# Rounding v and scaling the probabilities on ScalarE in a two-layer hybrid decoder trunk

## Chip, core and metric

The kernel runs on one core of one Trainium2 chip. The metric is the device time of one execution in microseconds (us): 2591.58 us, the median of three runs (2588.98 to 2593.63).

The engines are named as in the profile: PE is TensorE (its weight loads are PEld), DVE is VectorE, ACT is ScalarE, POOL is GpSimd, SP is SyncE, which here issues nearly all DMAs. Each engine works through its own queue in order and waits on semaphores for the others.

## What is computed

Two decoder layers over 512 tokens of width 1024, all in float32. Each layer is a half-step feed-forward block, a token mixer and another half-step feed-forward block. The mixer has three branches, and the change lies in the first two:

```python
proj = h @ w_in                       # q, k, v for both kinds of heads, and u for the convolution
# A: 8 dilated heads of 64; q and k RMS-normed; one combined masked softmax
p = jnp.exp(logits - m)
o = jnp.einsum('...qk,...kc->...qc', p, v) / den
# B: 4 differential heads; two softmaxes for one v of 128
p = jax.nn.softmax(logits, axis=-1)
a = p[:, :, 0] - lam * p[:, :, 1]
out = jnp.einsum('bhqk,bhkd->bhqd', a, v)
# C: causal depthwise convolution with 31 taps over u, LayerNorm, swish
y = sum_i sigmoid(h @ w_gate_i + b_i) * (branch_i @ w_branch_i)
x = x + g2 * (y @ w_out)
```

## The kernel before

**Matmuls.** Every float32 product is made of three matmuls on rounded halves: each operand is split into a high part (rounded to fp32r) and a low part (operand minus high part), and high·high, low·high and high·low are added in PSUM. Weights come from HBM through SP into the buffers `wr`; ACT rounds them to `wh` (L226) and DVE subtracts to get `wl` (L230). Activations are split the same way (L268 on ACT, L269 on DVE).

**The mixer of a layer.** Eight groups `i` are worked one after the other: groups 0 to 3 hold two A heads each, groups 4 to 7 one B head each. They are called units here (unit 0 is group 0). `project` (L816) makes q, k and v of a unit: four PSUM banks `mm`, one per 128 tokens, with 96 matmuls each 384 wide. When a bank is complete, ACT copies its q and k to `qk` (L840), and v (128x128) is split into `v[:, 0]`, the rounded part (L841), and `v[:, 1]`, the rest (L842, on DVE). A bank can be reused by the next unit's projection only when L840, L841 and L842 have read it; there are four such banks. `qk_norm` then normalises q and k (DVE: L855 to L861).

**Attention** (`attention`, L908) handles a unit in four blocks of 128 queries, n = 0 to 3, each with w = 128 (n+1) keys. `scores` (L885) makes two score tiles, one per A head or one per softmax of a B head. DVE adds the bias and finds the maximum (L902), ACT takes the exponential in place and sums it into `den` (L904), and DVE takes the reciprocal `rd` (L920). In an A unit both tiles are multiplied by their reciprocals (L924). In a B unit the second reciprocal is first multiplied by minus lambda (L926), the second tile by that (L927), and the first tile is scaled and added (L928). After that PE transposes the tiles (L937), they are split into `pT` (L268, L269), and `pv` (L964) or `sc` (L979, L982) multiplies them with both parts of v.

**What runs beside it.** PE fills its time with the next unit's projection, `pull(n)` taking n matmuls of it at a time. Each pull also advances the convolution: 4 x 31 taps, each one DVE instruction on 128x512 (L770). For the first three of four channel groups one tap is issued every 4 pulls, for the last one every 14. All of it is written in program order and then put into a fixed order per engine when the program is built; on the chip each engine's queue is in that order.

Of the kernel before, what the change touches and what calls it, by code (L numbers as in the profile page):

```python
# [16 lines left out]
AF = mybir.ActivationFunctionType  # L17
ALU = mybir.AluOpType
# [55 lines left out]
class Trunk:  # L74
# [741 lines left out]
    def project(self, l, i, st):  # L816

        nc, io = self.nc, self.io
        ps = [self.bank("mm") for _ in range(4)]
        for sub in range(4):  # L820
            if sub == 3:
                st["qk"] = qk = self.t4k([P, 4, 256], F32, "qk")
                st["v"] = v = self.t4k([P, 2, 4, P], F32R, "v")
            w = self.weight("qkv", l, i, sub)
            for t in range(4):
                for kk in range(2):
                    k = sub * 2 + kk
                    hs = slice(t * P, (t + 1) * P)
                    ws = slice(kk * 384, (kk + 1) * 384)
                    hi, lo = self.h[k]  # L830
                    o = ps[t][:, 0:384]
                    nc.tensor.matmul(o, hi[:, hs], w[0][:, ws], start=k == 0, stop=False)  # L832
                    yield
                    nc.tensor.matmul(o, hi[:, hs], w[1][:, ws], start=False, stop=False)  # L834
                    yield
                    nc.tensor.matmul(o, lo[:, hs], w[0][:, ws], start=False, stop=k == KD - 1)  # L836
                    if k < KD - 1:
                        yield
                if sub == 3:
                    nc.scalar.activation(qk[:, t, :], ps[t][:, 0:256], AF.Copy)  # L840
                    nc.vector.tensor_copy(v[:, 0, t, :], ps[t][:, 256:384])  # L841
                    nc.vector.tensor_tensor(v[:, 1, t, :], ps[t][:, 256:384],  # L842
                                            v[:, 0, t, :].bitcast(F32), op=ALU.subtract)
                    if t == 3:
                        self.qk_norm(l, i, st)
                    yield
# [61 lines left out]
    def attention(self, l, i, st, ys, pull, before):  # L908
        nc = self.nc
# [5 lines left out]
        def sa(n):  # L915
            w = (n + 1) * P
            e0, e1 = self.scores(st, (0, 1), (0, 1) if A else (0, 0), n,
                                 (den[:, 2 * n:2 * n + 1], den[:, 2 * n + 1:2 * n + 2]), pull)
            rd = self.small(2, "rd")
            nc.vector.reciprocal(rd, den[:, 2 * n:2 * n + 2])  # L920
            if A:
                dat[n] = [e0, e1]
                for j, e in enumerate(dat[n]):
                    nc.vector.tensor_scalar(e[:, 0:w], e[:, 0:w], rd[:, j:j + 1], None, op0=ALU.mult)  # L924
                return
            nc.vector.tensor_tensor(rd[:, 1:2], rd[:, 1:2], self.neglam[:, l:l + 1], op=ALU.mult)  # L926
            nc.vector.tensor_scalar(e1[:, 0:w], e1[:, 0:w], rd[:, 1:2], None, op0=ALU.mult)  # L927
            nc.vector.scalar_tensor_tensor(e0[:, 0:w], e0[:, 0:w], rd[:, 0:1], e1[:, 0:w],  # L928
                                           op0=ALU.mult, op1=ALU.add)
            dat[n] = [e0]  # L930
# [96 lines left out]
        for n, upto in enumerate((24, 29, 48, 65, 77, 96) if A else (22, 40, 53, 63, 86, 108)):  # L1027
            if n < 4:
                sa(n)
            if n == 0 and before:  # L1030
                pull(13)
                before()
            if not A:
                pull(12)
            for j in range(2 if A else 1):
                if A and n in (3, 5) and j == 0:
                    pv(n // 2 - 1)
                if not A and 0 <= n - 2 < 4:
                    sc(n - 2)
                if 0 <= n - 1 < 4:  # L1040
                    left = base + upto - pull.count
                    pull(max(0, left // (4 - j) if A else left - 2))
                    sb(n - 1, j)
            pull_to(upto)
# [200 lines left out]
```

## Time and profile before

| | us |
|---|---|
| median of three runs | 2591.58 |
| the profiled execution | 2593.34 |
| its span, first to last instruction | 2591.2 |
| layer 0: units 0 to 3 (the A heads) | 478.3 to 618.6 |
| layer 1: units 0 to 3 | 1758.1 to 1900.1 |
| TensorE's mean granted clock, share of 2.4 GHz | 0.987 |

A unit is taken here from the start of its first L902 on 128x128 to that of the next unit's. The span holds two mixers of some 400 us each and four feed-forward blocks around them. A busy time is the time in which at least one instruction of the engine ran. Instructions of DVE and ACT overlap their successors a little, so the distance from one start to the next is somewhat shorter than a duration. The clock column of a stretch is a mean of two levels, 1.2 and 2.4 GHz.

### The profile page before, as it was taken

The page shows a single profiled execution, that of the slowest core. Times are in us where ns is not written, and L with a number is a line of the kernel's source. Part 1 is how long each engine was busy: PE and PEld are TensorE (multiplying, and loading weights), DVE is VectorE, ACT ScalarE, POOL GpSimd, SP SyncE. Part 2 cuts the span into 40 slices and gives each one's busy share as a digit, 9 for nine tenths or more (in the row PEclk, how much of TensorE's full clock was granted, in tenths as well). Part 3 has the DMA queues.
Part 4 walks back from the last instruction along what each step waited for, and adds up shares of the span by engine and source line. Part 5 has one row for each costly group of instructions (what it writes and reads, how often), then busy time and mean ns, then how long its engine had stood idle before and what let it go on. Part 6 is the DMA issues. An engine that isn't in the chain of part 4 may idle for free.

```text
span 2591.2 us, 37974 instructions
## 1 busy us (share of the span) xinstructions
PE 2505.5 (97%) x15072; PEld 2201.5 (85%) x15072; DVE 1968.4 (76%) x3519; ACT 1124.6 (43%) x1765; POOL 30.5 (1%) x33
## 2 busy tenths in 40 slices
PE   6899999989999999999989999999899999999999
PEld 4889898877778889898989898898787778898988
DVE  8988876989873468979678796679898744785855
ACT  4435343545562345343455353435455523552533
POOL 2000000000000000000000000000000000000000
PEclk9999999989999999999999999999899999999999
DMA  7474644212223323737324553331122232233332
GB/s 264 163 244 158 236 149 127 80 46 76 78 90 98 90 74 98 260 107 260 107 65 157 209 183 123 96 88 54 50 81 78 90 94 93 66 106 98 101 97 89
DMA packets 97747, 312.20 MB, mean 120 GB/s; under 512 B 10345, under 2 KB 17257, under 8 KB 97570
## 3 DMA queue, kind: packets, MB, share of 16 engines
q1 hardware_dynamic: 97424, 309.65, 37.1%
q8 instruction: 118, 1.93, 0.3%
q14 instruction: 59, 0.48, 0.1%
q10 hardware_dynamic: 146, 0.14, 0.0%
HBM read 307.62 MB, written 6.06 MB: 121 GB/s over the span
## 4 chain that ended last, share of the span: by engine, by line
PE 82%; DVE 12%; ACT 3%; issue 2%; DMA 1%; SPq 0%; DVEq 0%; ACTq 0%
PE mm L583 16%; PE mm L274 13%; PE mm L276 13%; PE mm L278 13%; PE s L583 12%; PE mm L834 3%; PE mm L832 3%; PE mm L836 3%; DVE wr L770 2%; PE s L895 2%; DVE wl L230 2%; DVE ada L431 1%; DMA ada<-in_w_ada 1%; PE o L964 1%; DVE hx L491 1%
## 5 line engine op out<-in xcount | busy, mean ns | idle before, releaser
L226 ACT ACTIVATE wh<-wr 128x1024 fp32r<-128x1024 f32 (+1 forms) x481 | 485.2, 1010 | 641.6 <-PE mm L278 303.0
L230 DVE TENSOR_TENSOR wl<-wr,wh 128x1024 fp32r<-128x1024 f32 (+1 forms) x468 | 544.7, 1166 | 238.3 <-ACT wh L226 237.1
L274 PE MATMUL mm<-ah,wh 128*128 128x512 f32 (+1 forms) x752 | 287.1, 383 | 0.0
L274 PE MATMUL mm<-hh,wh 128*128 128x512 f32 (+1 forms) x776 | 281.6, 366 | 5.7 <-ACT wh L226 2.9
L278 PE MATMUL mm<-al,wh 128*128 128x512 f32 (+1 forms) x752 | 286.7, 382 | 0.0
L276 PE MATMUL mm<-hh,wl 128*128 128x512 f32 (+1 forms) x776 | 281.5, 366 | 5.2 <-DVE wl L230 5.2
L276 PE MATMUL mm<-ah,wl 128*128 128x512 f32 (+1 forms) x752 | 286.4, 382 | 0.0
L583 PE MATMUL mm<-sh,wh 128*128 128x256 f32 x936 | 268.4, 287 | 16.6 <-ACT wh L226 13.9
L278 PE MATMUL mm<-hl,wh 128*128 128x512 f32 (+1 forms) x776 | 276.5, 367 | 7.2 <-DVE hl L500 7.1
L583 PE MATMUL mm<-sh,wl 128*128 128x256 f32 x936 | 268.0, 286 | 0.5 <-DVE wl L230 0.5
L583 PE MATMUL mm<-sl,wh 128*128 128x256 f32 x936 | 267.7, 286 | 0.0
L509 DVE SCALAR_TENSOR_TENSOR x<-mm,res,x 128x512 f32<-128x512 f32 (+1 forms) x124 | 86.2, 697 | 156.2 <-PE mm L278 156.0
L583 PEld LDWEIGHTS mm<-sh,wh 128*128 128x128 f32 x936 | 182.1, 195 | 18.6 <-ACT wh L226 14.7
L834 PE MATMUL mm<-wl,hh 128*128 128x384 f32 x512 | 183.8, 359 | 8.5 <-DVE wl L230 8.5
L832 PE MATMUL mm<-wh,hh 128*128 128x384 f32 x512 | 177.3, 360 | 8.7 <-DVE v L842 8.7
L583 PEld LDWEIGHTS mm<-sh,wl 128*128 128x128 f32 x936 | 182.5, 195 | 1.2 <-DVE wl L230 0.8
L836 PE MATMUL mm<-wh,hl 128*128 128x384 f32 x512 | 183.5, 358 | 0.0
L583 PEld LDWEIGHTS mm<-sl,wh 128*128 128x128 f32 x936 | 182.6, 195 | 0.0
L770 DVE SCALAR_TENSOR_TENSOR wr<-u,par,wr 128x512 f32<-128x512 f32 x240 | 176.1, 744 | 0.2
L431 DVE SCALAR_TENSOR_TENSOR ada<-ada,cb 128x1024 f32<-128x1024 f32 x144 | 173.1, 1219 | 3.1 <-DMA ada<-in_w_ada 2.9
L274 PEld LDWEIGHTS mm<-hh,wh 128*128 128x128 f32 x776 | 147.6, 191 | 32.5 <-ACT hh L493 4.1
L583 PE MATMUL s<-hl,wh 128*128 128x256 f32 x624 | 175.1, 281 | 0.0
(218 smaller groups left out, 5603.8 us busy)
## 6 DMA issues: line engine op xcount, KB each, us to landing
wr<-in_w_up SPq DMA_DIRECT2D x156, 512.0 KB, 3.7
ada<-in_w_ada SPq DMA_DIRECT2D x144, 512.0 KB, 5.7
wr<-in_w_down SPq DMA_DIRECT2D x64, 512.0 KB, 5.4
wr<-in_w_qkv SPq DMA_DIRECT2D x64, 384.0 KB, 3.2
wr<-in_w_gate SPq DMA_DIRECT2D x48, 512.0 KB, 3.7
wr<-in_w_down SPq DMA_DIRECT2D x32, 384.0 KB, 3.1
wr<-in_w_branch SPq DMA_DIRECT2D x24, 512.0 KB, 3.6
wr<-in_w_u SPq DMA_DIRECT2D x16, 512.0 KB, 3.6
```

The costliest lines, as they stand in the source:

```text
L226: nc.scalar.activation(hi[:, :n], raw[:, :n], AF.Copy)
L230: eng.tensor_tensor(lo[:, :n], raw[:, :n], hi[:, :n].bitcast(F32), op=ALU.subtract)
L274: nc.tensor.matmul(ps[:, rng], w[0][:, wcol], ah[:, rng], start=start, stop=False)
L276: nc.tensor.matmul(ps[:, rng], w[1][:, wcol], ah[:, rng], start=False, stop=False)
L278: nc.tensor.matmul(ps[:, rng], w[0][:, wcol], al[:, rng], start=False, stop=stop)
L431: nc.vector.scalar_tensor_tensor(w, w, 1.0, cb, op0=ALU.mult, op1=ALU.mult, accum_out=self.mod[l][:, e:e + 1])
L509: self.nc.vector.scalar_tensor_tensor(self.x[d][:, rng], ps[:, rng], self.res[l][:, 8 * s + d:8 * s + d + 1], self.x[d][:, rng], op0=ALU.m ...
L583: nc.tensor.matmul(o, w[a][:, c], acts[k][b], start=first and (mi, k, x) == (0, 0, 0), stop=(k, x) == (3, 2), skip_group_check=True)
L770: nc.vector.scalar_tensor_tensor(ca[j], u, w, ca[j], op0=ALU.mult, op1=ALU.add)
L832: nc.tensor.matmul(o, hi[:, hs], w[0][:, ws], start=k == 0, stop=False)
L834: nc.tensor.matmul(o, hi[:, hs], w[1][:, ws], start=False, stop=False)
L836: nc.tensor.matmul(o, lo[:, hs], w[0][:, ws], start=False, stop=k == KD - 1)
```

## The change

Three lines of code move from VectorE to ScalarE: the rounding of v to its high part (64 instructions of 128x128), the scaling of both A tiles by their reciprocals (64 instructions, 16 each of 128, 256, 384 and 512 columns), and the scaling of the second B tile (32 instructions, 8 of each width). The values computed are the same products and roundings.

```diff
                 if sub == 3:
                     nc.scalar.activation(qk[:, t, :], ps[t][:, 0:256], AF.Copy)
-                    nc.vector.tensor_copy(v[:, 0, t, :], ps[t][:, 256:384])
+                    nc.scalar.activation(v[:, 0, t, :], ps[t][:, 256:384], AF.Copy)
...
                 for j, e in enumerate(dat[n]):
-                    nc.vector.tensor_scalar(e[:, 0:w], e[:, 0:w], rd[:, j:j + 1], None, op0=ALU.mult)
+                    nc.scalar.activation(e[:, 0:w], e[:, 0:w], AF.Copy, scale=rd[:, j:j + 1])
                 return
             nc.vector.tensor_tensor(rd[:, 1:2], rd[:, 1:2], self.neglam[:, l:l + 1], op=ALU.mult)
-            nc.vector.tensor_scalar(e1[:, 0:w], e1[:, 0:w], rd[:, 1:2], None, op0=ALU.mult)
+            nc.scalar.activation(e1[:, 0:w], e1[:, 0:w], AF.Copy, scale=rd[:, 1:2])
```

Since the order per engine is made anew when the program is built, it moves in other places of the mixers too, on PE, DVE, ACT and (the bias loads `G`) SP. The number of table loads on ACT is 32 in both programs.

First, DVE in layer 0 at the end of unit 1, where the banks of unit 3's projection are emptied. `mm_4985` and `mm_4986` are the first two of its four banks, `v_5235` its v, `qT` the split q and k of unit 2, `wl` a weight's low part and the `wr` rows are taps of the convolution:

```order
 L881 SCALAR_TENSOR_TENSOR qT_5231<-s_5226,par,qT_5231 128x512
 L230 TENSOR_TENSOR wl_5239<-wr_5236,wh_5238 128x768
 L770 SCALAR_TENSOR_TENSOR wr_4357<-u_4103,par,wr_4357 128x512
-L841 CAST v_5235<-mm_4985 128x128
-L770 SCALAR_TENSOR_TENSOR wr_4357<-u_4103,par,wr_4357 128x512
 L842 TENSOR_TENSOR v_5235<-mm_4985,v_5235 128x128
 L770 SCALAR_TENSOR_TENSOR wr_4357<-u_4103,par,wr_4357 128x512
-L841 CAST v_5235<-mm_4986 128x128
-L770 SCALAR_TENSOR_TENSOR wr_4357<-u_4103,par,wr_4357 128x512
 L842 TENSOR_TENSOR v_5235<-mm_4986,v_5235 128x128
+L770 SCALAR_TENSOR_TENSOR wr_4357<-u_4103,par,wr_4357 128x512
```

The subtraction that frees the first bank stands behind one tap in place of a tap, the rounding and a second tap.

Second, ACT in unit 2 of layer 0, query blocks n = 1 (`p_5345`, `p_5349`) and n = 2 (`p_5392`, `p_5396`):

```order
 L904 ACTIVATE p_5349,den_5215<-p_5349,m_5350 128x256
 L268 ACTIVATE pT_5359<-s_5375 128x128
+L924 ACTIVATE p_5345<-p_5345,rd_5353 128x256
+L924 ACTIVATE p_5349<-p_5349,rd_5353 128x256
 L268 ACTIVATE pT_5359<-s_5409 128x2x128
 L904 ACTIVATE p_5392,den_5215<-p_5392,m_5393 128x384
 L268 ACTIVATE pT_5359<-s_5419 128x2x128
 L904 ACTIVATE p_5396,den_5215<-p_5396,m_5397 128x384
+L924 ACTIVATE p_5392<-p_5392,rd_5400 128x384
+L924 ACTIVATE p_5396<-p_5396,rd_5400 128x384
```

Two scalings now stand between a pair of exponentials and the next work of ACT; each waits for a reciprocal of DVE.

Third, DVE in the first B unit of layer 0 (unit 4, n = 0; `p_6016` and `p_6020` are the two softmaxes, `v_5977` is the v of the next unit):

```order
 L855 TENSOR_REDUCE ss_6043<-sq_6044 128x4
-L842 TENSOR_TENSOR v_5977<-mm_5742,v_5977 128x128
-L230 TENSOR_TENSOR wl_6082<-wr_6079,wh_6081 128x768
-L920 RECIPROCAL rd_6024<-den_5957 128x2
-L841 CAST v_5977<-mm_5743 128x128
-L926 TENSOR_TENSOR rd_6024<-rd_6024,neglam 128x1
 L855 TENSOR_REDUCE ss_6043<-sq_6047 128x4
-L927 TENSOR_SCALAR p_6020<-p_6020,rd_6024 128x128
-L842 TENSOR_TENSOR v_5977<-mm_5743,v_5977 128x128
 L928 SCALAR_TENSOR_TENSOR p_6016<-p_6016,rd_6024,p_6020 128x128
```

L928 now waits for ACT where it followed L927 on its own engine; the reciprocal and L926 have moved further ahead of it.

## Rows read from the trace of the kernel before

**Rows 1.** The page, busy time, share of the span and instructions of each engine:

```profile
PE 2505.5 (97%) x15072; PEld 2201.5 (85%) x15072; DVE 1968.4 (76%) x3519; ACT 1124.6 (43%) x1765; POOL 30.5 (1%) x33
```

**Rows 2.** Busy time by stretch, units 0 to 3 of layer 0:

```profile
core 0: us, PE busy (x) PEld busy (x) DVE busy (x) ACT busy (x) POOL busy (x), PEclk, DMA share, GB/s
478.30:509.00 30.70, 29.38 (x165) 24.31 (x164) 28.48 (x89) 18.46 (x48) 0.00 (x0) 1.00 0.17 51
509.00:547.30 38.30, 33.90 (x182) 27.80 (x183) 36.59 (x101) 18.24 (x49) 0.00 (x0) 0.96 0.18 50
547.30:589.60 42.30, 36.04 (x171) 29.61 (x170) 37.19 (x101) 16.67 (x46) 0.00 (x0) 0.86 0.17 50
589.60:618.60 29.00, 27.74 (x152) 23.09 (x153) 26.25 (x84) 15.17 (x43) 0.00 (x0) 0.96 0.22 63
```

**Rows 3.** The same columns, units 0 to 3 of layer 1:

```profile
1758.10:1788.80 30.70, 29.37 (x165) 24.33 (x164) 28.49 (x89) 18.49 (x48) 0.00 (x0) 1.00 0.18 51
1788.80:1827.10 38.30, 33.91 (x182) 27.83 (x183) 36.59 (x101) 18.12 (x49) 0.00 (x0) 0.96 0.17 50
1827.10:1869.60 42.50, 36.22 (x171) 29.76 (x170) 37.25 (x102) 16.68 (x46) 0.00 (x0) 0.86 0.17 49
1869.60:1900.10 30.50, 29.25 (x153) 24.52 (x154) 26.23 (x85) 15.20 (x43) 0.00 (x0) 0.90 0.21 61
```

**Rows 4.** Chain that ended last, 528 to 546 us: start, us, what:

```profile
528.54 0.79 DVE p L924 x2
...
543.06 0.87 DVE wl L230
543.92 0.66 DVE wr L770
544.59 0.20 DVE v L841
544.79 0.66 DVE wr L770
545.45 0.21 DVE v L842
```

**Rows 5.** PE in order of time: start, us, instruction, idle time before it and releaser:

```profile
545.80 0.66 PE L832 MATMUL mm<-wh,hh 128*128 128x384 f32 x1 [1.84 <-DVE v L842]
...
546.57 0.52 PE L836 MATMUL mm<-wh,hl 128*128 128x384 f32 x1
546.89 0.52 PE L832 MATMUL mm<-wh,hh 128*128 128x384 f32 x1
...
557.42 0.34 PE L834 MATMUL mm<-wl,hh 128*128 128x384 f32 x1
557.59 0.34 PE L836 MATMUL mm<-wh,hl 128*128 128x384 f32 x1
```

**Rows 6.** Busy time by stretch of L841 (first) and L924 (second) alone, unit 1:

```profile
509.00:547.30 38.30, 1.14 (x4) 0.96 0.18 50
...
509.00:547.30 38.30, 2.78 (x8) 0.96 0.18 50
```

**Rows 7.** Groups by line and shape: count, busy us, mean ns of one, idle before; last, line L924:

```profile
L841 DVE CAST v<-mm 128x128 fp32r<-128x128 f32 x64 | 17.5, 282 | 0.0
L904 ACT ACTIVATE p<-p,m 128x512 f32<-128x512 f32 x32 | 22.9, 716 | 3.2 <-DVE m L902 3.2
L904 ACT ACTIVATE p<-p,m 128x128 f32<-128x128 f32 x32 | 12.6, 395 | 22.6 <-DVE m L902 18.5 <-DVE rs L313 4.0
L268 ACT ACTIVATE pT<-s 128x128 fp32r<-128x128 f32 x40 | 10.9, 272 | 19.4 <-PE s L937 15.4 <-DVE pT L269 3.7
L226 ACT ACTIVATE wh<-wr 128x768 fp32r<-128x768 f32 x104 | 87.1, 843 | 155.7 <-PE mm L836 66.4 <-PE mm L278 38.3 <-issue 32.4
L924 DVE TENSOR_SCALAR p<-p,rd x64: 274/380/481, 481.7 to 1888.2; 128x128 f32<-128x128 f32 x16, 128x256 f32<-128x256 f32 x16, 128x384 f32<-128x384 f32 x16, 128x512 f32<-128x512 f32 x16
```

**Rows 8.** Busy time by stretch, units 4 and 5 of layer 0, and 690 to 700 us:

```profile
618.60:649.60 31.00, 31.00 (x181) 26.86 (x181) 29.50 (x98) 16.39 (x42) 0.00 (x0) 1.00 0.26 78
649.60:687.80 38.20, 38.19 (x202) 30.81 (x201) 36.08 (x113) 18.18 (x39) 0.00 (x0) 1.00 0.26 77
690.00:700.00 10.00, 8.55 (x42) 5.70 (x41) 8.25 (x22) 7.52 (x13) 0.00 (x0) 1.00 0.39 120
```

## Prediction

> **What bounds the kernel now.** I read the page's busy shares first: PE is busy 97% of the span and ACT 43% [rows 1]. Taken alone that says that a change on DVE and ACT is worth nothing. The share is an average, though, so the second view is the busy time of each unit of the mixer. In units 0 to 3 of layer 0 PE stands idle for 30.70-29.38 = 1.3, 38.30-33.90 = 4.4, 42.30-36.04 = 6.3 and 29.00-27.74 = 1.3 us, 13.2 us in all [rows 2]. In the same stretches the granted clock is 0.96 to 0.86 of 2.4 GHz in three of the four. A stretch of 38.3 us at a mean of 0.96 has lost 1.5 us of full-speed time, the others 5.9 and 1.2, together 8.6. Layer 1 repeats it: 13.2 us idle, and 1.5 + 6.0 + 3.1 = 10.6 us of clock [rows 3]. So these eight units lose 45.6 us of PE's time, and that is all that the change can win there; in units 4 and 5 PE has no gap at all [rows 8].
>
> Who holds PE up is read from DVE's column and from the chain. In units 1 and 2 DVE is busy 36.59 of 38.30 and 37.19 of 42.30 us, ACT less than half [rows 2]. The chain that ended last runs through DVE at the end of unit 1: two scalings, later a weight's low part, a tap, the rounding of v, another tap, the subtraction [rows 4]. Behind that PE has waited 1.84 us for L842, the last reader of a bank that the next projection needs. The wide matmuls after it start 0.32 us apart, where later ones start 0.17 apart [rows 5]: the wait costs a second time, as a stretch at 1.2 GHz. So DVE, with the taps on top of the attention, is the limit in units 1 and 2. In unit 3 the taps come at the slower rate, and DVE is busy 26.25 of 29.00 us.
>
> **What the change takes from DVE.** Per A unit four roundings and eight scalings go: 1.14 + 2.78 = 3.92 us of DVE busy time in unit 1 [rows 6]; the other units are within 0.2. That is the upper bound, since neighbours overlap. In the chain two scalings of 512 columns take 0.79 and a rounding 0.20 [rows 4], against 0.28 for the rounding's duration [rows 7], so about 0.08 of each of the 12 is overlap: the lower bound is 3.9-1.0 = 2.9. I take the middle, 3.4 us.
>
> **What ACT gets.** The trace has no multiplication by a column on ACT from SBUF to SBUF. The nearest row is the exponential in place with a column as its bias: 0.395 us at 128 columns, 0.716 at 512 [rows 7], the upper bound for this operation; a rounding of 128x128 from PSUM takes 0.272 there, and v's is the same. Eight scalings of 0.56 on average (half-way between the two) and four roundings are 4.4 + 1.1 = 5.5 us per A unit. ACT is busy 18.2 of 38.3 us in unit 1, so it would go to 23.7 us: it has the room. As engine time alone it costs nothing, covered by ACT's idle time, and where that cover is gone it is 5.5 us a unit.
>
> Here a rule speaks against the change. On DVE a scaling takes 0.27 to 0.48 us, and the row of an exponential in the same shape says 0.4 to 0.7 on ACT [rows 7]. The Trainium skill, "ScalarE: Activation LUTs", section "Rules for kernel authors", wants multiplications on VectorE, not ScalarE; the trace agrees that each one gets dearer. By that rule, ACT being the bound, each unit would lose some 5.5 us; by the row that DVE is the full engine it gains.
>
> **The sum.** The work that PE has in unit 1 is 38.3-4.4-1.5 = 32.4 us, in unit 2 42.3-6.3-5.9 = 30.1. DVE's work after the change is 36.6-3.4 = 33.2 and 37.2-3.4 = 33.8: still a little more than PE's, so DVE stays the limit of these two units, with less over. I leave it the 1.7 us of idle time it has in unit 1 now, waits for other engines, in both. The unit then takes 34.9 and 35.5 us: gains of 3.4 and 6.8 us. The second is larger because the slow clock, which makes DVE wait for PE now, goes with the long waits. Units 0 and 3 are bound by PE; of their 1.3 us of gaps each I take half, and unit 3's 1.2 us of slow clock in part: 0.7 and 0.8. Layer 0 gains 11.7 us. Layer 1 has the same units with 42.5 us in unit 2 (gain 7.0) and more slow clock in unit 3, which follows unit 2's waits (2.1): 0.7 + 3.4 + 7.0 + 2.1 = 13.2. Together 24.9.
>
> **What it adds.** In the A units the scaling waits on ACT for a reciprocal of DVE. Queued behind it on ACT are the copies of the transposed tiles, the next exponentials and, in places, `wh` and the copies of q, k and v; PE waits for all of them. In the new order the reciprocal stands right behind the exponentials, with a tap or less between, so I take this as covered by DVE's smaller backlog. The roundings go behind L840 in ACT's queue, and L842 waits for them in place of its neighbour; with 0.27 us each and two taps fewer in front of the first subtraction, nothing is added.
>
> In the B units, one scaling per block leaves DVE, and L928 waits for it there. DVE loses about 2 us of work per unit (four scalings and four roundings, half to two thirds of an A unit's), which is worth nothing where PE has no gap [rows 8]. Below, then, zero. Above, each of the 32 waits lasts a whole `wh` of 0.84 us and a scaling of 0.72 [rows 7], 6.2 us per unit; DVE's free time is 1.5 and 2.1 us in units 4 and 5 plus those 2 us, so some 2.5 us per unit would come through, 20 us over eight units. The new order puts other DVE work between L926 and L928, so I take the row near the bottom: 1 us per layer, at the place where PE already waits in this stretch (8.55 of 10 us, ACT 7.52 busy) [rows 8]. Table loads stay 32 and cost nothing new. The bias loads that SP issues in another order move by one weight load and are wanted a unit later: nothing.
>
> 24.9-2.0 = 22.9 us. Against the profiled execution's own 2593.3 us that is 2570.4; that execution stands 1.8 us above the median of the runs, so 2568.7, rounded **2569 us**.
>
> **The rivals.** First, **ACT's queue becomes the slow link** (slower). The place is the pair of scalings in each of the 32 blocks of A units, 16 per layer. If the reciprocal sits behind taps in DVE's backlog, ACT stands still at the scaling, and the copies that PE needs stand behind it. One tap is 0.66 us [rows 4]: at one per block 21 us, about the whole gain; at two 42 us, which gives 2570 + 42 = 2612, or 2611 in the median. It decides from 22.9/32 = 0.7 us per block. For it: the exponentials already wait mostly for DVE's maximum (18.5 of the 22.6 us before the 128-wide ones) [rows 7]. Against it: the reciprocal's place in the new order, and that the backlog is what shrinks. Chance 0.11. The Trainium skill's rule above is this case; the trace bears out its price per instruction, not that ACT is the bound.
>
> Second, **DVE's time is given back as waits**. L842 and L920 now wait for ACT more often; if DVE's idle time per unit grows by the 3.4 us that it was relieved of, units 1 and 2 stay at 38.3 and 42.3; units 0 and 3 still give 1.5 us a layer, the B units take 1: 2591, within 0.2%. For it: in unit 2 DVE is idle for 5.1 us now. Against: those lie in the slow-clock stretch. Chance 0.12.
>
> Third, **half of it**: unit 1 gains, but one wait of PE's in unit 2 stays long enough for the clock to fall as it does now, 5.9 us. Then a layer gains 3.4 + 0.9 + 1.5 = 5.8 us, less 1: 9.6 us in all, 2582. Chance 0.17.
>
> Fourth, **the whole loss goes**: the relief brings DVE's work under PE's everywhere, since over the four units it falls to 128.5-13.6 = 114.9 us against PE's 140.3-13.2-8.6 = 118.5. All 45.6 us: 2546; nine tenths of it, 2551. Chance 0.10. That the change doesn't do what it says can be left out: the three lines stand on ACT in the new order.
>
> **How the numbers follow.** The forecast, a gain of 13 to 33 us, has 0.50. A measurement of this kernel tells about 0.2%, 5.2 us, from no change. Faster: 0.50 + 0.17 + 0.10 = 0.77; within: 0.12; slower: 0.11. The range runs from 2552, leaving out some 0.07 below, to 2591, leaving out the slower case and a little of the second rival above.
>
> **What would show it.** In the changed profile DVE's busy time in units 1 and 2 of both layers should be near 33 to 34 us, PE's wait for L842 at the start of unit 2 gone, the granted clock at 0.98 or above there, and units 1 and 2 near 35 us. ACT should be near 24 us busy in them. A wait of ACT's for L920 of over 0.7 us per block would show the first rival; DVE waiting for L841 or L927 the second; a stretch with matmuls 0.32 us apart the third. PE below full in units 4 and 5 would show the B units' cost. The prediction is wrong if units 1 and 2 keep their lengths although DVE's work fell, or if the time goes in a place outside the A units.

## The result, and the profile after

The change takes 2561.02 us, the median of four runs (2559.45 to 2561.60), against 2592.28 us before (four runs, 2588.98 to 2593.63): a ratio of 0.988, 95% interval 0.9863 to 0.9897, or 31.3 us faster. The prediction was 2569 us in 2552 to 2591: right in its sign and its place, and too small by 8 us. The profiled execution of the changed kernel took 2559.45 us, with a span of 2557.4 and a mean granted clock of 0.995 of 2.4 GHz (before: 0.987).

The page's busy shares, to be read beside [rows 1]:

```profile
PE 2492.0 (97%) x15072; PEld 2188.8 (86%) x15072; DVE 1929.6 (75%) x3359; ACT 1177.0 (46%) x1925; POOL 30.5 (1%) x33
```

160 instructions have gone from DVE to ACT, 39 us of DVE's busy time has gone and 52 us of ACT's has come, and PE's share has not moved. The page alone still hides the change; the stretches show it. These are units 0 to 5 of layer 0 in the changed kernel, to be read beside [rows 2] and [rows 8]:

```profile
core 0: us, PE busy (x) PEld busy (x) DVE busy (x) ACT busy (x) POOL busy (x), PEclk, DMA share, GB/s
477.70:508.20 30.50, 30.33 (x170) 25.33 (x171) 27.35 (x79) 20.94 (x58) 0.00 (x0) 1.00 0.18 55
508.20:540.70 32.50, 32.50 (x178) 26.41 (x177) 30.23 (x84) 22.10 (x63) 0.00 (x0) 1.00 0.22 61
540.70:576.20 35.50, 32.03 (x179) 26.66 (x177) 34.47 (x90) 22.02 (x60) 0.00 (x0) 1.00 0.20 57
576.20:603.10 26.90, 26.82 (x146) 21.71 (x145) 23.95 (x73) 18.70 (x52) 0.00 (x0) 1.00 0.25 69
603.10:634.20 31.10, 31.10 (x180) 26.66 (x179) 29.28 (x89) 19.62 (x52) 0.00 (x0) 1.00 0.25 77
634.20:672.00 37.80, 37.24 (x198) 30.03 (x197) 35.80 (x110) 20.65 (x47) 0.00 (x0) 1.00 0.27 78
```

And units 1 to 3 of layer 1, beside [rows 3]:

```profile
1769.60:1802.10 32.50, 32.50 (x178) 26.42 (x177) 30.23 (x84) 22.12 (x63) 0.00 (x0) 1.00 0.23 61
1802.10:1837.60 35.50, 32.01 (x173) 26.68 (x172) 34.46 (x90) 22.00 (x60) 0.00 (x0) 0.96 0.19 56
1837.60:1865.90 28.30, 28.29 (x152) 23.21 (x152) 24.02 (x74) 18.72 (x52) 0.00 (x0) 0.98 0.25 67
```

Against before, units 0 to 3 of layer 0 are 0.2, 5.8, 6.8 and 2.1 us shorter, 14.9 together, and those of layer 1 0.2, 5.8, 7.0 and 2.2, 15.2 together: 30.1 of the 31.3 us lie in the A units. (The two profiled spans differ by 33.8; the executions profiled lie 2.5 us further apart than the medians.) In unit 1 PE has no gap left, in unit 2 still 3.5 us in each layer. Units 4 and 5 are as they were, to 0.4 us. A unit's start is a mark on DVE, and PE's order around it has changed too, so a tenth of a microsecond in such a difference means nothing.

At the start of unit 2, where PE waited 1.84 us for L842 [rows 5], nothing waits now. PE there, in order of time:

```profile
540.17 0.44 PE L832 MATMUL mm<-wh,hh 128*128 128x384 f32 x1
540.45 0.34 PE L834 MATMUL mm<-wl,hh 128*128 128x384 f32 x1
540.62 0.34 PE L836 MATMUL mm<-wh,hl 128*128 128x384 f32 x1
```

The matmuls start 0.17 us apart, the pace of 2.4 GHz, where [rows 5] had 0.32. DVE's queue just before, beside [rows 4]:

```profile
537.43 0.95 DVE L230 TENSOR_TENSOR wl<-wr,wh 128x768 fp32r<-128x768 f32 x1
538.30 0.74 DVE L770 SCALAR_TENSOR_TENSOR wr<-u,par,wr 128x512 f32<-128x512 f32 x1
538.96 0.28 DVE L842 TENSOR_TENSOR v<-mm,v 128x128 fp32r<-128x128 f32 x1
```

The first subtraction starts 1.53 us after the weight's low part; before it was 545.45 - 543.06 = 2.39 [rows 4]. The 0.86 us between them is the rounding (0.20) and the tap behind it (0.66). That turned out to be a large part of the story.

### The profile page after: what moved, and what is told of

Same layout as the page of the kernel before. It is cut to its first block, busy times and chain, and to the rows that moved or that the text cites. A ratio compares the mean times of both kernels' runs of the same rounds, so it can differ in the third digit from the quotient of the medians.

```text
span 2557.4 us, 37996 instructions
## 1 busy us (share of the span) xinstructions
PE 2492.0 (97%) x15072; PEld 2188.8 (86%) x15072; DVE 1929.6 (75%) x3359; ACT 1177.0 (46%) x1925; POOL 30.5 (1%) x33
## 4 chain that ended last, share of the span: by engine, by line
PE 86%; DVE 9%; ACT 2%; issue 1%; DMA 1%; DVEq 0%; ACTq 0%
PE mm L583 17%; PE mm L274 14%; PE mm L278 14%; PE mm L276 14%; PE s L583 13%; PE mm L836 3%; PE mm L834 3%; PE mm L832 3%; PE s L895 2%; DVE wl L230 1%; DVE wr L770 1%; PE o L964 1%; PE s L937 1%; DVE ada L431 1%; DVE hx L491 1%
## 5 line engine op out<-in xcount | busy, mean ns | idle before, releaser
L226 ACT ACTIVATE wh<-wr 128x1024 fp32r<-128x1024 f32 (+1 forms) x481 | 485.8, 1011 | 617.0 <-PE mm L278 294.7
L230 DVE TENSOR_TENSOR wl<-wr,wh 128x1024 fp32r<-128x1024 f32 (+1 forms) x468 | 544.0, 1165 | 235.5 <-ACT wh L226 234.4
L770 DVE SCALAR_TENSOR_TENSOR wr<-u,par,wr 128x512 f32<-128x512 f32 x240 | 175.1, 742 | 0.3
L583 PE MATMUL s<-hh,wh 128*128 128x256 f32 x624 | 174.8, 280 | 0.0
```

The source lines that it names most:

```text
L226: nc.scalar.activation(hi[:, :n], raw[:, :n], AF.Copy)
L230: eng.tensor_tensor(lo[:, :n], raw[:, :n], hi[:, :n].bitcast(F32), op=ALU.subtract)
L583: nc.tensor.matmul(o, w[a][:, c], acts[k][b], start=first and (mi, k, x) == (0, 0, 0), stop=(k, x) == (3, 2), skip_group_check=True)
L770: nc.vector.scalar_tensor_tensor(ca[j], u, w, ca[j], op0=ALU.mult, op1=ALU.add)
```

## The experiments

Each kernel was run in several rounds beside the kernel before, whose median was 2590.14 us in the first group of runs, 2591.12 in the second and 2591.51 in the third. Where a line is added to the kernel, its result goes to a scratch tile and is overwritten before anything reads it. The theory was the prediction's: DVE's load in units 1 and 2 is what the change removes.

### The three parts apart

Only the rounding on ACT:

```diff
-                    nc.vector.tensor_copy(v[:, 0, t, :], ps[t][:, 256:384])
+                    nc.scalar.activation(v[:, 0, t, :], ps[t][:, 256:384], AF.Copy)
```

> Only the rounding of v goes to ACT; both scalings stay on DVE. Theory (DVE's work in units 1 and 2 sets the time): DVE loses about 1.0 us per A unit of the 3.9 that the whole change takes, so about a quarter of the 31 us: 2582 to 2587 against 2592, and units 1 and 2 of layer 0 still longer than 36 and 39 us. Rival (the freed banks matter, not DVE's load): the wait of PE for L842 is what the rounding's place in the queue sets, so this edit alone gives most of the gain, 2570 or less.

Measured: 2574.34 us, ratio 0.994 [0.9924, 0.9957], 15.8 us faster. The theory gave it 5 to 10 us and the rival 22 or more; neither had it right. Units 1 and 2 of layer 0 took 35.8 and 38.7 us, where the theory wanted over 36 and 39. No other expectation of a time here missed.

Only the scaling of the A tiles:

```diff
-                    nc.vector.tensor_scalar(e[:, 0:w], e[:, 0:w], rd[:, j:j + 1], None, op0=ALU.mult)
+                    nc.scalar.activation(e[:, 0:w], e[:, 0:w], AF.Copy, scale=rd[:, j:j + 1])
```

> Only the scaling of the A tiles goes to ACT. Theory: 2.8 of the 3.9 us per A unit leave DVE, so most of the gain, 2566 to 2574. Rival (the banks): little, 2586 or more. Rival (waits of ACT for the reciprocal eat it up): no gain, 2590 or more, with over 0.7 us of ACT's idle time per block in front of L924.

Measured: 2568.52 us, 0.9912 [0.9897, 0.9927], 21.6 us faster, as expected. PE's waits for L842 stay (4.6 us in the mixer of layer 0, 4.3 before), and ACT waits for the reciprocals 0.2 us per block (6.5 us in all).

Only the scaling of the second B tile (L927):

```diff
-            nc.vector.tensor_scalar(e1[:, 0:w], e1[:, 0:w], rd[:, 1:2], None, op0=ALU.mult)
+            nc.scalar.activation(e1[:, 0:w], e1[:, 0:w], AF.Copy, scale=rd[:, 1:2])
```

> Only the scaling of the second B tile goes to ACT. Theory: PE has no gap in units 4 and 5, so nothing is won or lost beyond 3 us: 2589 to 2595. Rival (DVE's waits for ACT in the B units cost time that the A units' gain hides in the whole change): 2598 or more. Rival (any new order of the engines moves the time by this much): some other time, more than 6 us away from 2592.

Measured: 2590.33 us, 1.000 [0.9991, 1.001]: nothing either way beyond some 2.5 us. The parts do not add up: 15.8 + 21.6 = 37.4 is more than the 31.3 of the whole. The overlap lies in the A units: those of layer 0 get 9.5 and 10.1 us shorter by the two parts alone, 19.6 together, and 14.9 by the whole. Why it is as large as that was not tried.

### The load put back

The whole change, with DVE doing as much as before: a copy of v's columns of the bank, and scalings of another tile by the same reciprocals.

```diff
                     nc.scalar.activation(v[:, 0, t, :], ps[t][:, 256:384], AF.Copy)
+                    nc.vector.tensor_copy(self.sq7[:, 0:P], ps[t][:, 256:384])
...
+                    nc.vector.tensor_scalar(self.sq7[:, 0:w], self.x[0][:, 0:w], rd[:, j:j + 1], None, op0=ALU.mult)
...
+            nc.vector.tensor_scalar(self.sq7[:, 0:w], self.x[0][:, 0:w], rd[:, 1:2], None, op0=ALU.mult)
```

> All three steps on ACT as in the change, but DVE gets back what it lost: a rounding of the same PSUM columns and scalings of the same widths by the same reciprocals, written to a tile that nobody reads then. Theory (the relief of DVE is the cause): the gain is gone, 2588 to 2600, units 1 and 2 back near 38 and 42 us, and the slow clock with them. Rival (the gain comes from the new order or from earlier work on ACT): 2561 to 2570.

Measured: 2595.37 us, 1.0017 [1.0007, 1.0026]. The gain is gone, and 5 us more, although ACT has the work. So the gain comes from what left DVE's queue; which part of it, the next runs tell. The loss does not lie quite where it was: units 1 and 2 of layer 0 take 37.4 and 39.1 us, at clocks of 0.97 and 0.89, and unit 0 takes 34.5 (30.7 before). The scaling of the A tiles alone, its load put back:

```diff
                 for j, e in enumerate(dat[n]):
-                    nc.vector.tensor_scalar(e[:, 0:w], e[:, 0:w], rd[:, j:j + 1], None, op0=ALU.mult)
+                    nc.scalar.activation(e[:, 0:w], e[:, 0:w], AF.Copy, scale=rd[:, j:j + 1])
+                    nc.vector.tensor_scalar(self.sq7[:, 0:w], self.x[0][:, 0:w], rd[:, j:j + 1], None, op0=ALU.mult)
```

> The scaling of the A tiles on ACT alone, and DVE does scalings of the same widths by the same reciprocals into a tile that nobody reads then. If the 21.6 us of the A scaling come from DVE's load, 2586 to 2596. If they come from the earlier or later finish of the scaled tiles or the order around it, 2567 to 2576.

Measured: 2590.17 us, 0.999 [0.998, 1.000]. Units 1 and 2 of layer 0 in this kernel, in the columns above:

```profile
510.80:548.90 38.10, 33.79 (x182) 27.87 (x183) 36.46 (x101) 22.08 (x57) 0.00 (x0) 0.98 0.18 50
548.90:588.80 39.90, 33.40 (x171) 27.39 (x170) 37.11 (x102) 20.77 (x54) 0.00 (x0) 0.93 0.18 53
```

DVE is as full as before (36.59 and 37.19 in [rows 2]), and the time is that of the kernel before. Whether the product that PE waits for is made on DVE or on ACT does not matter; the 21.6 us of the scalings are DVE's load.

The whole change, with only the scalings' load put back (the second and third added lines of the first diff in this section):

> The whole change, and DVE gets back the load of both scalings, not that of the rounding. If the rounding's gain is the bank's and the scalings' gain is DVE's load, it comes out like the rounding alone, 2572 to 2580. If load counts for both, 2580 to 2588. If load counts for neither, 2558 to 2566.

Measured: 2576.16 us, 0.9937 [0.9922, 0.9952]: the rounding's gain, 15 us, and nothing else.

### Why the rounding is worth so much

First its load: the rounding goes to ACT, and DVE reads the rounded v once more, behind the subtraction.

```diff
-                    nc.vector.tensor_copy(v[:, 0, t, :], ps[t][:, 256:384])
+                    nc.scalar.activation(v[:, 0, t, :], ps[t][:, 256:384], AF.Copy)
                     nc.vector.tensor_tensor(v[:, 1, t, :], ps[t][:, 256:384],
                                             v[:, 0, t, :].bitcast(F32), op=ALU.subtract)
+                    nc.vector.tensor_copy(self.sq7[:, 0:P], v[:, 0, t, :].bitcast(F32))
```

> The rounding of v goes to ACT and both scalings stay on DVE, as in the run of the rounding alone, which gained 15.8 us for about 1.0 us of DVE's time per unit. DVE now gets that time back as a copy of the rounded v, behind the subtraction, so that the bank is free before it. If the 15.8 us came from DVE's load, 2586 to 2594. If they came from the bank's earlier release (one step of DVE's queue fewer in front of it), 2574 to 2580. In between, both.

Measured: 2575.78 us, 0.9945 [0.9925, 0.9965], 15.3 us faster. With three quarters of the load back (0.22 us a copy for the rounding's 0.28) the whole gain stays, so here the theory of load falls: in units 0 to 3 of layer 0 the load does cost (134.6 us together, 130.8 without it), but hardly any of that reaches the end (spans of 2571.6 and 2570.4 us). Then the place: a copy of the same size, but ahead of the subtraction, where the rounding stood.

```diff
-                    nc.vector.tensor_copy(v[:, 0, t, :], ps[t][:, 256:384])
+                    nc.scalar.activation(v[:, 0, t, :], ps[t][:, 256:384], AF.Copy)
+                    nc.vector.tensor_copy(self.sq7[:, 0:P], ps[t][:, 256:384])
                     nc.vector.tensor_tensor(v[:, 1, t, :], ps[t][:, 256:384],
                                             v[:, 0, t, :].bitcast(F32), op=ALU.subtract)
```

> The rounding of v on ACT, both scalings on DVE, and DVE makes a copy of the same PSUM columns where its rounding stood, ahead of the subtraction. Against the run with DVE's time given back behind the subtraction (2575.8) only the place of that instruction differs. If the bank's release is what the rounding costs, 2586 to 2594, as before the change. If the gain comes from something else that the rounding's move does (ACT's order, the new order elsewhere), 2572 to 2580.

Measured: 2590.34 us, 0.9994 [0.9985, 1.0003]. The gain is gone. The two kernels differ in that line (its place, and whether it reads the bank or v) and in the order that is built from it. What the copy reads matters little: 0.20 us from its start to the next with the bank, 0.14 with v. DVE's queue shows what the place does. DVE at the end of unit 1, with the copy behind the subtraction (there the copy is L844):

```profile
541.92 0.95 DVE L230 TENSOR_TENSOR wl<-wr,wh 128x768 fp32r<-128x768 f32 x1
542.79 0.75 DVE L770 SCALAR_TENSOR_TENSOR wr<-u,par,wr 128x512 f32<-128x512 f32 x1
543.45 0.28 DVE L842 TENSOR_TENSOR v<-mm,v 128x128 fp32r<-128x128 f32 x1
...
544.31 0.22 DVE L844 COPY sq<-v 128x128 f32<-128x128 f32 x1
```

PE in the same kernel, with the idle time before the matmul and its releaser:

```profile
543.88 0.41 PE L832 MATMUL mm<-wh,hh 128*128 128x384 f32 x1 [0.97 <-DVE v L842]
```

DVE with the copy ahead of the subtraction (the copy is L842 there and the subtraction L843):

```profile
543.71 0.95 DVE L230 TENSOR_TENSOR wl<-wr,wh 128x768 fp32r<-128x768 f32 x1
544.58 0.74 DVE L770 SCALAR_TENSOR_TENSOR wr<-u,par,wr 128x512 f32<-128x512 f32 x1
545.24 0.28 DVE L842 COPY sq<-mm 128x128 f32<-128x128 f32 x1
545.44 0.74 DVE L770 SCALAR_TENSOR_TENSOR wr<-u,par,wr 128x512 f32<-128x512 f32 x1
546.10 0.28 DVE L843 TENSOR_TENSOR v<-mm,v 128x128 fp32r<-128x128 f32 x1
```

And PE in that one:

```profile
546.53 0.56 PE L832 MATMUL mm<-wh,hh 128*128 128x384 f32 x1 [1.83 <-DVE v L843]
```

An instruction of 0.20 us ahead of the bank's last reader brings a tap of 0.66 with it, and PE's wait grows by the sum of the two, from 0.97 to 1.83 us. At the end of unit 2 the same two kernels have waits of 1.65 and 2.50 us. First the copy behind the subtraction, then ahead of it:

```profile
582.98 0.41 PE L832 MATMUL mm<-wh,hh 128*128 128x384 f32 x1 [1.65 <-DVE v L842]
586.28 0.42 PE L832 MATMUL mm<-wh,hh 128*128 128x384 f32 x1 [2.50 <-DVE v L843]
```

Unit 3 in the two, in the same order (length, clock, DMA):

```profile
585.70:612.30 26.60, 1.00 0.25 70
588.20:618.90 30.70, 0.90 0.23 61
```

In the second, PE's matmuls start 0.32 us apart soon behind that wait. Units 0 to 6 of layer 0 take 243.5 and 251.1 us, those of layer 1 243.4 and 253.3. Of the 7.6 us in layer 0, 1.7 are the two waits, and 3.6 the clock: 0.8 + 3.2 + 3.1 us lost in units 1 to 3 (one minus the clock, times the length) against 0.7 + 2.8. The other 2.3 lie in units 4 to 6 (111.1 against 108.9 us) and were not followed further: the rest of the order is built anew for each kernel too. A kernel with the rounding left on DVE and only the tap behind it moved was not run, so what the rounding costs there without the tap stays open.

### Is ACT near its limit?

The whole change, with every moved step done a second time on ACT:

```diff
                     nc.scalar.activation(v[:, 0, t, :], ps[t][:, 256:384], AF.Copy)
+                    nc.scalar.activation(self.sq7[:, 0:P], ps[t][:, 256:384], AF.Copy)
...
+                    nc.scalar.activation(self.sq7[:, 0:w], self.x[0][:, 0:w], AF.Copy, scale=rd[:, j:j + 1])
...
+            nc.scalar.activation(self.sq7[:, 0:w], self.x[0][:, 0:w], AF.Copy, scale=rd[:, 1:2])
```

> The changed kernel with each of the moved steps done twice on ACT: a second rounding of the same columns and a second scaling by the same reciprocals, into a tile that nobody reads then. ACT gets about 5 us more per A unit, 22 to 27 of 32.5 us. Theory (ACT has the room): 2561 to 2570. Rival (ACT is close to being the bound, as where multiplications are wanted on VectorE): 2580 or more.

Measured: 2564.14 us, 0.9896 [0.9881, 0.9911], 3 us above the change's median, or 4 us by the two ratios. 160 more instructions, 50 us of ACT's time (1227.1 against 1177.0 on the page), cost about that much and no more. ACT's queue is not the bound, and the first rival falls by experiment as well as by its row below.

### How much of the loss can go?

The taps are the rest of DVE's load in units 1 and 2. Issuing one every 5 pulls in place of 4 moves some of them later, without any change in their number:

```diff
-                yield 4 if j < 3 else 14
+                yield 5 if j < 3 else 14
```

In the kernel before:

> The kernel before with the convolution's taps of the first three channel groups issued every 5 pulls in place of 4, nothing else. Theory (DVE is overfull in units 1 and 2 because of the taps): DVE gets about 3.3 us fewer taps per unit there, as much as the change takes from it, and more in unit 3, which has room: a gain of 10 to 25 us, 2567 to 2582. Rival (what counts is how soon the roundings and scalings are done): 2588 or more.

Measured: 2581.09 us, 0.996 [0.9946, 0.9975], 10 us faster. In the changed kernel:

> The changed kernel with the taps every 5 pulls. Theory: what PE still loses is 3.5 us of idle time in unit 2 of each layer and some slow clock in layer 1; about half of it goes, 2553 to 2559, unless unit 3 becomes too full (23.95 us of 26.9 now, plus some 7). Rival (DVE is no limit any more): 2561 within 3 us.

Measured: 2556.60 us, 0.9865 [0.985, 0.988]. Units 0 to 3 of layer 0 in it:

```profile
478.20:507.80 29.60, 29.60 (x167) 24.89 (x167) 27.29 (x78) 21.01 (x59) 0.00 (x0) 1.00 0.26 75
507.80:537.40 29.60, 29.60 (x167) 24.88 (x168) 27.62 (x79) 20.80 (x58) 0.00 (x0) 1.00 0.22 65
537.40:567.50 30.10, 30.10 (x169) 25.04 (x169) 27.90 (x79) 20.48 (x57) 0.00 (x0) 1.00 0.18 53
567.50:598.90 31.40, 31.24 (x177) 25.93 (x175) 28.86 (x82) 22.07 (x63) 0.00 (x0) 1.00 0.17 47
```

PE is full and the clock whole: next to nothing is lost in the A units any more, which take 4.7 us less than with the change alone in layer 0 and 6.1 less in layer 1. Yet the whole is only 4.4 us faster, and the intervals overlap. Unit 7 of layer 0 starts 7.5 us earlier than in the changed kernel, but unit 0 of layer 1 starts at 1740.0 against 1739.1 us: all of it is given back in between. Measured at the same matmul, the lead is down to 3.7 us at 795 us, before the mixer has ended. In part that is no loss, since PE has more work behind the start of unit 7 (up to that matmul it is busy 83.4 of 85.3 us, against 80.6 of 81.5). Then 2.0 us go in the feed-forward block behind the mixer, and 2.1 near 1130 us, where PE waits twice for a weight's low part (1.5 us). This is 930 to 970 us in the changed kernel:

```profile
930.00:970.00 40.00, 34.81 (x256) 32.33 (x256) 36.93 (x72) 28.46 (x52) 2.41 (x1) 1.00 0.17 53
```

And in the one with a tap every 5 pulls, which is 3.8 us ahead at the start of this stretch and 1.8 at its end:

```profile
930.00:970.00 40.00, 33.96 (x230) 32.04 (x231) 35.22 (x68) 26.60 (x46) 0.00 (x0) 0.90 0.17 53
```

PE waits for the same weights there in both (once 2.6 us for L226 in the changed kernel and 2.8 in this one, then 1.6 for L230 and 1.3 for L226 in both), but here the granted clock falls to 0.90 behind them. Last, the rounding and the A scalings on ACT, the B scaling left on DVE, and a tap every 5 pulls:

> A version to use: rounding of v and A scalings on ACT, the B scaling left on DVE, taps every 5 pulls. Theory (the B scaling gives nothing): as the changed kernel with taps every 5 pulls, 2552 to 2560. Rival (the B scaling helps where the taps come later and fill DVE in the B units): 2562 or more.

Measured: 2555.79 us, 0.9857 [0.9842, 0.9871]. That is the best of all, by less than can be told from the one above it: L927 on ACT is worth nothing here either.

## Why the prediction was right, and where it was off

**What bounds the kernel** was read rightly. Before, units 1 and 2 were held up by DVE, and the loss lay in PE's waits and in the slow clock behind them. Put all of DVE's work back where it stood and the gain is gone; give ACT twice the work and nearly all of it stays.

**The relief** of 3.4 us per A unit was right, but not all of DVE's drop is that. The busy time and count of the taps alone (L770), unit 1 of the kernel before:

```profile
509.00:547.30 38.30, 16.42 (x23) 0.96 0.18 50
```

The same of the changed kernel:

```profile
508.20:540.70 32.50, 13.91 (x20) 1.00 0.22 61
```

DVE's busy time in unit 1 fell by 36.59 - 30.23 = 6.4 us. 2.5 of it are three taps that now come in other units, which leaves 3.9, the upper bound. In unit 2 it fell by 2.7 with two taps (0.6 us) more. The prediction expected 33 to 34 us in both and had not looked at where the new order puts the taps; hence unit 1 at 32.5 us where it said 34.9. There PE, busy all of the 32.50 us, is the limit now, and not DVE as the text had it. Unit 2 came out at 35.5, as predicted, but with luck: DVE was busy 34.5 us there where the sum had 33.8, and idle for 1.0 where the sum left it 1.7.

**The term that was mis-sized** is the rounding. It stood in the sum as 1.1 of 3.9 us of relief [rows 6], 29% of 24.9 us or some 7; measured alone it brings 15.8, and on top of the scalings still 31.3 - 21.6 = 9.7. The text had the chain in front of it (rounding, tap, subtraction [rows 4]) and said of the new order "two taps fewer in front of the first subtraction", but used that only to cost the wait for ACT at nothing. (By the order it is one tap fewer: a tap, the rounding and a second tap stood there before, one tap after.) It should have been priced: 0.86 us less wait at the end of units 1 and 2 of each layer, and with shorter waits less slow clock behind them. The three taps that left unit 1 go with it too: with the rounding alone on ACT unit 1 has 20 taps, with the A scalings alone 23 as before. The scalings, at 71% of 24.9 or 18 us, were nearly well sized (21.6).

By units, the 8.4 us between the gain of 22.9 in the sum and the 31.3 measured are these: 4.8 in unit 1 (5.8 a layer for 3.4), 1.4 in unit 3 (2.1 and 2.2 for 0.8 and 2.1), nothing in unit 2, 1.0 the other way in unit 0 (0.2 a layer for 0.7), and 3.2 outside the A units, where 2.0 were set aside as a loss and 1.2 came as a gain (by the medians; the two profiled executions put 2.5 more there).

**The B units' cost** of 2 us came by half at most. DVE does wait for ACT there, 5.1 us in 8 of the 32 blocks, as the row of L928's idle time shows; of PE's time 1.0 us goes to waiting for L928:

```profile
  ACT p L927: 5.1, 8
  PE s L937: 1.0, 2
```

That is 0.5 us in unit 7 of each layer, and not at 690 to 700 us, where the text put it: the wait of 1.45 us for L226 that PE had there has gone. In units 4 and 5 PE is busy 31.10 of 31.10 us and 37.24 of 37.80. The 0.6 us missing in unit 5, the text's own sign of this cost, are waits for L881 and L1003, and the unit is no longer than before. The scaling of the B tile alone moved the time by nothing that could be told from noise. The first choice in the text, that time off DVE is worth nothing where PE has no gap, holds for most of the time that DVE now stands waiting too.

**What ACT gets** was nearly right: 5.5 us per unit were estimated. The group of L924 in the changed kernel, with min, median and max ns of one:

```profile
L924 ACT ACTIVATE p<-p,rd x64: 386/554/728, 481.3 to 1853.8; 128x128 f32<-128x128 f32 x16, 128x256 f32<-128x256 f32 x16, 128x384 f32<-128x384 f32 x16, 128x512 f32<-128x512 f32 x16
```

Its busy time in unit 1, by stretch:

```profile
508.20:540.70 32.50, 4.03 (x8) 1.00 0.22 61
```

With four roundings of 0.272 us that makes 4.03 + 1.09 = 5.1 us. ACT's busy time in units 1 and 2 came to 22.1 and 22.0 us, a little under the 24 that the text gave as a sign.

The exponential's rows of 395 to 716 ns [rows 7] were the price, not the upper bound.

**The rivals.** The first needed 0.7 us of ACT waiting per block. ACT's waits in units 0 to 3 of layer 0 (us, times, longest) say 1.9 us over 16 blocks, 0.12 per block:

```profile
ACT p L924 <- DVE rd L920: 1.9, 4, 0.8
```

The Trainium skill's rule in "ScalarE: Activation LUTs", section "Rules for kernel authors", which would keep the multiplications on VectorE, has the dearer engine right (a median of 554 ns here against 380 on DVE [rows 7]). The measurement decides against it here, since the dearer engine is the one with time to spare. The second rival (DVE's time given back as waits) needed 3.4 us more idle time of DVE per unit; it is 2.3 us in unit 1 (1.7 before) and 1.0 in unit 2 (5.1 before). The third (the clock falls all the same) is alive in part: PE's waits on DVE in the mixer of layer 0 are now

```profile
PE mm L832 <- DVE v L842: 1.6, 1, 1.6
PE mm L834 <- DVE wl L230: 1.2, 1, 1.2
```

both in unit 2, and in layer 1 the clock dips behind the first. The fourth (all 45.6 us) was open: the taps show that nearly all of the loss in the A units can go, but a good part then comes back elsewhere.

## What to carry to other kernels

Price a moved instruction twice: by the time that it takes on its engine, and by what stands behind it in that engine's queue. Ahead of the last reader of a buffer that the bounding engine waits for, it can be worth twice what its share of the load would give (here 15.8 us alone for 7), above all where a filler instruction has settled between the two. And look at which units the fillers fall into after the order is rebuilt, before forecasting a unit's length.

## What the runs showed of the hardware

The same wait of PE's need not cost the same. In the changed kernel PE waits 1.64 us for L842 at the end of unit 2 in both layers, behind the same instructions. PE there in layer 0, and then in layer 1:

```profile
573.82 0.42 PE L832 MATMUL mm<-wh,hh 128*128 128x384 f32 x1 [1.64 <-DVE v L842]
574.08 0.34 PE L834 MATMUL mm<-wl,hh 128*128 128x384 f32 x1
574.25 0.34 PE L836 MATMUL mm<-wh,hl 128*128 128x384 f32 x1
```

```profile
1835.21 0.66 PE L832 MATMUL mm<-wh,hh 128*128 128x384 f32 x1 [1.64 <-DVE v L842]
1835.67 0.52 PE L834 MATMUL mm<-wl,hh 128*128 128x384 f32 x1
1835.99 0.52 PE L836 MATMUL mm<-wh,hl 128*128 128x384 f32 x1
```

In layer 0 the matmuls start 0.17 us apart at once, in layer 1 0.32 apart, 1.2 GHz, until 1838.2. So a wait of this length may or may not bring the clock down, and a forecast has to leave some 1.4 us open for each such wait (nine matmuls, each 0.15 us longer). Five of the traced kernels have this wait at the end of unit 2 in both layers (the change, the rounding alone, the rounding with its load behind the subtraction, the scalings' load put back, ACT's work twice): behind three of the ten waits the granted clock fell. Six have 2.5 us there (before, each scaling alone, the A scalings with their load, the copy ahead of the subtraction, the whole load put back): behind all twelve it fell within 2 us, for 3 to 7 us.

Shorter waits may do it too. With 0.27 and 0.98 us of waiting close together at the end of unit 1, the wide matmuls stay 0.17 us apart where the rounding alone is on ACT, and start 0.32 apart from 545 us where the scalings' load is put back.
